# The S5 setup's and tables' transfers on GpSimd's queue instead of SyncE's

## The chip, the cores and the metric

The kernel runs on one core of a Trainium2 chip. A core has five engines that run side by side, each with its own in-order list of instructions: TensorE (PE in the profile; its weight loads are PEld), VectorE (DVE), ScalarE (ACT), GpSimd (POOL) and SyncE (SP). An engine that issues a DMA puts it into its own list; if that DMA has to wait for data or for a buffer, everything behind it in the list waits too. The metric is device microseconds for one execution, lower being better.

## The reference

One layer of a hybrid decoder over 2048 tokens of width 1024, in float32: an RMSNorm, one wide input projection, three branches and a gated merge.

```
h = rms_norm(x) * norm_w
ua, za, q, k, v, zb, xbc, dt, zc, g = split(h @ w_in)
ya = s5_mixer(ua, ...)                      # diagonal complex state space, 32 groups of 16 channels, 64 states
yb = dilated_window_attention(norm(q), norm(k), v)   # 3 pairs of (window, dilation)
yc = ssd(conv(xbc), dt, ...)                # chunked scan of Mamba-2
y  = sum(sigmoid(g_i) * (silu-gated y_i @ proj_i)) @ w_out + x
```

What the change touches belongs to `s5_mixer`. Its recurrence is linear, so that the response of a group to 8 steps of input can be tabulated from the parameters alone:

```
step = exp(log_step);  lam = exp((a_re + i a_im) * step)
bb = ((lam - 1) / a) * b
bu = einsum(bb, u);  h_t = lam * h_(t-1) + bu_t
y  = Re(c h) + d * u
```

Nothing in these tables depends on the tokens, only on `a`, `b`, `c`, `d` and `log_step`.

## The kernel before, in words

Every float32 matmul is done as three in the type fp32r: an operand is split into a high half (a cast on ACT, `wh_*`, `hT_hi`) and a low half (a subtraction on DVE, `wl_*`, `hT_lo`), and high × high, low × high and high × low are summed (L398 to L400 and L409 to L411). So PE needs four tensors made by ACT and DVE before it can go through a piece of the projection.

The 2048 tokens are handled in two halves of 1024. For each half the projections run over pieces of w_in's columns, and one matmul group is a unit. `main` (L1545 and on) hands side jobs to ranges of units: `s5_setup` to units 2 to 38, `s5_tables` to units 41 to 86, attention of the first half beside the tables, the first half's chunked scan (SSD) to units 89 to 135. PE's projection matmuls are the steady work that all side jobs hide behind.

The program's start is `a0` (L311): eight token tiles, each loaded as two DMAs (`load_x`, L280), squared on ACT (L289), its two sums added on DVE (L290), its inverse root taken on POOL (`rsqrt`, L248 and L249, tile `xs`), scaled on DVE (L297), transposed on PE (L301, `xT`), and split into `hT_hi` (ACT, L330) and `hT_lo` (DVE, L331). `consts` (L206 to L243) loads small constants, among them the convolution's weights `convw` (L241, L242, scaled on DVE in L243). `a0_early` does tiles 8 to 15 later, in the same way except that the result goes to DRAM (L343). The norms of the attention heads (`ss_q`, `ss_k`) use the same `rsqrt` on POOL, and their scaled results go out through L442.

`s5_setup` (L1066) loads the parameters (13 DMAs: four `s5ld`, one `s5prm`, four `s5b`, four `s5c`), computes powers and phases on DVE, and puts ten pieces into a DRAM table `tab_d` through the helper `put` (L1083), and `rho_d`. `s5_tables` (L1235) loads `s5dd` once and then goes through 16 blocks of two groups. A block loads its table rows (`s5t`, L1246), forms three complex products (`s5x`, `s5k`, `s5o`: two products each on POOL in L1261 and L1262, one sum on DVE in L1263), lets PE transpose `s5x` (`s5pp`, L1269) and multiply by `s5k` (`s5kp`, L1278), forms `s5w` (L1303 to L1305), and stores four results (`p_d`, `ks_d`, `o_d`, `wt_d`). The tile `s5t` has two buffers, so that a block's load can run one block ahead.

The order within each engine is not the order of the source text. The framework simulates the program on a timeline and writes each engine's list in the order in which that simulation issued the instructions; it also adds the waits. So a line that moves to another engine changes the order of all lists:

```
with tile.TileContext(nc, schedule_with_timeline_sim=True) as tc:
    Hybrid(tc, aps, out).build()
```

Completion of DMAs is signalled by eight semaphores for those that SP issues and another eight for those that POOL issues; a ninth transfer in flight waits for the first of its kind.

Of the kernel before, what the change touches and what calls it, by code (L numbers as in the profile page):

```python
# [21 lines left out]
P = 128  # L22
# [127 lines left out]
class Hybrid:  # L150
# [915 lines left out]
    def s5_setup(self):  # L1066


        nc, A = self.nc, self.A
        sm = Small(nc, self.jp, [P, 32])  # L1070
        prm = self.ct("s5prm", [P, 3, 32])
        ld = self.ct("s5ld", [32, 2, 2, 64])
        for i, w in enumerate(("s5_a_re", "s5_a_im")):
            for j in range(2):
                nc.sync.dma_start(ld[:, i, j, :], A[w][0])
        nc.sync.dma_start(prm[:, 2, :], A["s5_log_step"].partition_broadcast(P))
        pt = self.cps([P, 2, 32], "s5pt")
        for i in range(2):
            nc.tensor.transpose(pt[:, i, :], ld[:, i].rearrange("g j p -> g (j p)"), self.ident[:32, :32])
        nc.vector.tensor_copy(prm[:, 0:2, :], pt)  # L1080
        ar, ai = prm[:, 0, :], prm[:, 1, :]
        def put(off, wd, src):
            nc.sync.dma_start(self.tab_d[:, :, off * 2:(off + wd) * 2], src)  # L1083
        bb = [self.ct(f"s5b{i}", [P, 32, 16]) for i in range(2)]
        for i, (up, dn) in enumerate((("s5_b_re", "s5_b_im"), ("s5_b_im", "s5_b_re"))):
            nc.sync.dma_start(bb[i][0:64], A[up][0].rearrange("g p i -> p g i"))
            nc.sync.dma_start(bb[i][64:128], A[dn][0].rearrange("g p i -> p g i"))
        nc.vector.tensor_scalar(bb[1][0:64], bb[1][0:64], -1.0, None, op0=ALU.mult)
        yield
        step = sm.exp(prm[:, 2, :])  # L1090
# [2 lines left out]
        mag, cs, sn, fr, fi, ang, rho = (sv[:, i, :] for i in range(7))  # L1093
# [43 lines left out]
        mul(t, nr, ai)  # L1137
        sub(fi, fi, t)
        mul(fi, fi, den)
        nc.sync.dma_start(self.rho_d, rho)  # L1140
        w = self.ct("s5w", [P, 32, 18])
        nc.vector.tensor_copy(w[:, :, 0:9], lr)
        nc.vector.tensor_copy(w[:, :, 9:18], li)
        put(128, 18, w.rearrange("p (b g) k -> p b (g k)", b=16))
        w = self.ct("s5wr", [P, 32, 2, 8])
        for n in range(8):
            nc.vector.tensor_copy(w[:, :, 0, 7 - n], lr[:, :, n])
            nc.vector.tensor_copy(w[:, :, 1, 7 - n], li[:, :, n])
        put(146, 16, w.rearrange("p (b g) a n -> p b (g a n)", b=16))
        yield  # L1150

# [3 lines left out]
        for i in range(2):  # L1155
            o = self.ct(f"s5bb{i}", [P, 32, 16])
            t = self.ct(f"s5bt{i}", [P, 32, 16])
            mul(o, bb[i], b16(fr))
            mul(t, bb[1 - i], b16(fi))
            (sub if i else add)(o, o, t)  # L1160
            put(64 + 16 * i, 16, o.rearrange("p (b g) k -> p b (g k)", b=16))
        yield
        c = [self.ct(f"s5c{i}", [P, 4, 2, 64]) for i in range(2)]
        for i, w in enumerate(("s5_c_re", "s5_c_im")):
            src = A[w][0].rearrange("(b g) i p -> (g i) b p", g=8)
            nc.sync.dma_start(c[0][:, :, i, :], src)
            nc.sync.dma_start(c[1][:, :, 1 - i, :], src)
        nc.vector.tensor_scalar(c[0][:, :, 1, :], c[0][:, :, 1, :], -1.0, None, op0=ALU.mult)
        nc.vector.tensor_scalar(c[1], c[1], -1.0, None, op0=ALU.mult)
        for i in range(2):  # L1170
# [8 lines left out]
        for lev in range(2):  # L1179
# [5 lines left out]
            for k in range(7 if lev else 3):  # L1185
                if lev == 0 or k >= 3:
                    a, b = sm.t(), sm.t()
# [11 lines left out]
            n = 2  # L1199
            qr, qi = pr, pi  # L1200
            t = self.ct(f"s5pt{lev}", [P, 32, 16])
            while n < 16:
                a, b = sm.t(), sm.t()
# [31 lines left out]
    def s5_tables(self):  # L1235


        nc, A = self.nc, self.A
        v, gp = nc.vector, nc.gpsimd
        dd = self.tct("s5dd", [16, 32])  # L1240
        nc.sync.dma_start(dd, A["s5_d"][0].rearrange("(g i) -> i g", i=16))

        for b in range(16):
            gs = slice(b * 2, b * 2 + 2)
            w = self.tct(f"s5t{b}", [P, 2 * TABW], tag="s5tab", bufs=2)
            nc.sync.dma_start(w, self.tab_d[:, b, :])  # L1246

            def piece(off, wd=16):
                return w[:, off * 2:(off + wd) * 2].rearrange("p (g k) -> p g k", k=wd)
            pw, rev = piece(128, 18), piece(146)  # L1250
            b1, b2, d1, d2 = (piece(k) for k in (64, 80, 96, 112))

            def cplx(name, lr, li, x1, x2):

                o = self.tct(f"s5{name}{b}", [P, 2, 8, 16], tag="s5c", bufs=3)
                t = self.tct(f"s5{name}t{b}", [P, 2, 8, 16], tag="s5ct", bufs=2)

                def bc(k, x):
                    return (k.unsqueeze(3).to_broadcast([P, 2, 8, 16]),
                            x.unsqueeze(2).to_broadcast([P, 2, 8, 16]))  # L1260
                gp.tensor_mul(o, *bc(lr, x1))  # L1261
                gp.tensor_mul(t, *bc(li, x2))  # L1262
                v.tensor_add(o, o, t)  # L1263
                return o

            x1 = cplx("x", rev[:, :, 0:8], rev[:, :, 8:16], b1, b2)
            pp = self.cps([P, 2, P], f"s5pp{b}")
            for g in range(2):
                nc.tensor.transpose(pp[:, g, :], x1[:, g].rearrange("p n i -> p (n i)"), self.ident)  # L1269
            p1 = self.tct(f"s5p1{b}", [P, 2, P], tag="s5p1", bufs=1)  # L1270
            nc.scalar.copy(p1, pp)
            nc.sync.dma_start(self.p1_d[:, gs, :], p1)
            yield
            o0 = cplx("k", pw[:, :, 0:8], pw[:, :, 9:17], d1, d2)

            kp = self.cps([16, 2, P], f"s5kp{b}")
            for g in range(2):
                nc.tensor.matmul(kp[:, g, :], b1[:, g, :], o0[:, g].rearrange("p n i -> p (n i)"),  # L1278
                                 start=True, stop=True)
            ks = self.tct(f"s5ks{b}", [16, 2, 15, 16], tag="s5ks", bufs=1)  # L1280
            v.memset(ks[:, :, 0:7, :], 0.0)
            nc.scalar.copy(ks[:, :, 7:15, :].rearrange("p g n i -> p g (n i)"), kp)
            for g in range(2):
                v.scalar_tensor_tensor(ks[:, g, 7, :], self.ident[0:16, 0:16], dd[:, b * 2 + g:b * 2 + g + 1],
                                       ks[:, g, 7, :], op0=ALU.mult, op1=ALU.add)
            nc.sync.dma_start(self.ks_d[:, gs, :], ks.rearrange("p g n i -> p g (n i)"))
            yield
            o1 = cplx("o", pw[:, :, 1:9], pw[:, :, 10:18], d1, d2)
            nc.sync.dma_start(self.o1_d[:, gs, :], o1.rearrange("p g n i -> p g (n i)"))
            yield  # L1290
            wt = self.tct(f"s5w{b}", [P, 2, 2, 256], tag="s5w", bufs=1)
            tmp = self.tct(f"s5wt{b}", [P, 2, 256], tag="s5wt", bufs=1)

            def lo16(k):
                return piece(k).unsqueeze(2).to_broadcast([P, 2, 16, 16])

            def hi16(k):
                return piece(k).unsqueeze(3).to_broadcast([P, 2, 16, 16])

            def v16(a):  # L1300
                return a.rearrange("p g (a b) -> p g a b", b=16)
            for q, (x, y, f) in enumerate(((0, 16, v.tensor_sub), (16, 0, v.tensor_add))):
                gp.tensor_mul(v16(wt[:, :, q, :]), hi16(32), lo16(x))  # L1303
                gp.tensor_mul(v16(tmp), hi16(48), lo16(y))
                f(wt[:, :, q, :], wt[:, :, q, :], tmp)  # L1305
            nc.sync.dma_start(self.wt_d[:, gs], wt)
            yield

    def s5(self):
# [376 lines left out]
```

## Time and profile before

| what | value |
|---|---|
| median of 3 runs | 2508.95 us (2505.32 to 2513.44) |
| profiled execution | 2510.43 us |
| its span in the trace | 2508.4 us |
| mean granted clock of PE | 0.988 |
| DMA traffic | 457.65 MB in 449734 packets |
| DMAs of S5 setup and tables on SP's queue | 105 |

The profiled execution is one run; 2.0 us of its time lie around the span. The busy times of the engines count arithmetic only, so the time that an engine spends issuing a DMA is not in them. In the timeline a number in brackets at a row's end is the idle time of that engine just before the row, and the name behind it is what it waited for. "SPq" marks instructions of SP's list, DMA issues above all; the time in such a row is that of the issue, not of the transfer. "PEclk" is the share of PE's full clock that was granted in the stretch.

### The profile page before, as it was taken

The numbers are of one execution on the slowest core, as the hardware profiler recorded it, in microseconds if no ns is written. First come the engines' busy times: TensorE is split into PE (matmuls) and PEld (weight loads), VectorE is DVE, ScalarE is ACT, GpSimd is POOL, SyncE is SP. The second block draws the span as 40 slices with busy tenths as digits, with TensorE's granted clock in tenths as the row PEclk, the third lists the DMA queues.
The fourth block names the chain that finished last, engine by engine and source line by source line (L and its number), as shares of the span: only waits on it lengthen the run. The fifth ranks groups of instructions, "written<-read, shape, count | busy, mean of one in ns | idle before, by whom it ended". The sixth has DMA issues, their size and how long they took to land.

```text
span 2508.4 us, 40680 instructions
## 1 busy us (share of the span) xinstructions
PE 2426.4 (97%) x15072; PEld 2126.8 (85%) x15072; DVE 1436.5 (57%) x3104; ACT 836.6 (33%) x1780; POOL 722.8 (29%) x785
## 2 busy tenths in 40 slices
PE   8989999999999999999999999999999799999999
PEld 8989998788788888988999978878888578898888
DVE  6953467876767672577664566632334886552321
ACT  4223334543444343222243355542332312120100
POOL 2242233543344540245331000010110465422120
PEclk9999999999999999999999999999999899999999
DMA  7764543454544456466544567783343689898886
GB/s 165 111 166 139 163 124 128 139 168 131 155 140 123 125 170 195 113 183 169 156 154 140 166 204 211 239 269 106 114 130 108 209 281 314 292 304 292 297 285 221
DMA packets 449734, 457.65 MB, mean 182 GB/s; under 512 B 115585, under 2 KB 389505, under 8 KB 442369
## 3 DMA queue, kind: packets, MB, share of 16 engines
q1 hardware_dynamic: 449536, 455.06, 59.0%
q8 instruction: 119, 1.95, 0.3%
q14 instruction: 79, 0.64, 0.1%
HBM read 306.90 MB, written 148.06 MB: 181 GB/s over the span
## 4 chain that ended last, share of the span: by engine, by line
PE 68%; DMA 12%; DVE 10%; POOL 3%; SPq 3%; ACT 2%; issue 2%; ACTq 0%; DVEq 0%; POOLq 0%
PE fp L1500 3%; PE fp L1501 3%; PE fp L1502 3%; PE ps_g L410 3%; PE ps_g L409 3%; PE ps_g L411 3%; PE ao L874 2%; PE ps_uz L409 2%; PE ps_uz L411 2%; PE ps_uz L410 2%; PE op L1531 2%; PE op L1532 2%; PE op L1533 2%; PE psx_g L722 2%; PE psx_g L720 2%
## 5 line engine op out<-in xcount | busy, mean ns | idle before, releaser
L1013 POOL TENSOR_TENSOR sr<-tle,ahl 128x384 fp32r<-128x384 f32 x128 | 126.6, 1008 | 483.9 <-PE sd L1018 400.4
L1501 PE MATMUL fp<-fy_lo,fp 128*128 128x512 f32 x384 | 154.4, 402 | 6.5 <-DVE fy_lo L1473 6.5
L1500 PE MATMUL fp<-fy_hi,fp 128*128 128x512 f32 x384 | 156.7, 409 | 0.0
L409 PE MATMUL ps_g<-hT_hi,wh_g 128*128 128x512 f32 x384 | 155.4, 405 | 0.0
L410 PE MATMUL ps_g<-hT_lo,wh_g 128*128 128x512 f32 x384 | 154.3, 402 | 0.0
L411 PE MATMUL ps_g<-hT_hi,wl_g 128*128 128x512 f32 x384 | 154.1, 401 | 0.0
L1502 PE MATMUL fp<-fy_hi,fp 128*128 128x512 f32 x384 | 153.7, 400 | 0.0
L1531 PE MATMUL op<-fo,fm_hi 128*128 128x256 f32 x512 | 146.1, 286 | 4.7 <-DMA fo<-wo_d 4.7
L1505 POOL TENSOR_TENSOR fm<-fm,fg 128x512 f32<-128x512 f32 x64 | 86.7, 1355 | 218.1 <-DVE fg L1503 153.4
L1532 PE MATMUL op<-fo,fm_hi 128*128 128x256 f32 x512 | 144.8, 283 | 0.0
L1533 PE MATMUL op<-fo,fm_lo 128*128 128x256 f32 x512 | 144.5, 283 | 0.1
L409 PE MATMUL ps_xbc<-hT_hi,wh_xbc 128*128 128x512 f32 x320 | 130.0, 406 | 0.0
L411 PE MATMUL ps_xbc<-hT_hi,wl_xbc 128*128 128x512 f32 x320 | 128.9, 403 | 0.0
L410 PE MATMUL ps_xbc<-hT_lo,wh_xbc 128*128 128x512 f32 x320 | 127.9, 400 | 0.0
L853 ACT ACTIVATE sm<-sm,ml 128x256 f32<-128x256 f32 (+1 forms) x192 | 86.3, 451 | 119.9 <-DVE ml L851 113.5
L398 PE MATMUL ps_q<-wh_q,hT_hi 128*128 128x256 f32 x384 | 112.1, 293 | 7.5 <-ACT wh_q L385 7.4
L400 PE MATMUL ps_q<-wh_q,hT_lo 128*128 128x256 f32 x384 | 109.9, 287 | 3.9 <-DVE hT_lo L331 3.9
L399 PE MATMUL ps_v<-wl_v,hT_hi 128*128 128x256 f32 x384 | 108.5, 283 | 3.2 <-DVE wl_v L386 3.2
L399 PE MATMUL ps_q<-wl_q,hT_hi 128*128 128x256 f32 x384 | 110.0, 287 | 0.9 <-DVE wl_q L386 0.9
L398 PE MATMUL ps_v<-wh_v,hT_hi 128*128 128x256 f32 x384 | 109.6, 286 | 0.0
L398 PE MATMUL ps_k<-wh_k,hT_hi 128*128 128x256 f32 x384 | 108.7, 285 | 0.0
L399 PE MATMUL ps_k<-wl_k,hT_hi 128*128 128x256 f32 x384 | 108.2, 283 | 0.2 <-DVE wl_k L386 0.2
(477 smaller groups left out, 7579.5 us busy)
## 6 DMA issues: line engine op xcount, KB each, us to landing
fp<-pw_d SPq DMA_DIRECT2D x32, 1536.0 KB, 6.7
fo<-wo_d SPq DMA_DIRECT2D x16, 2048.0 KB, 9.0
fg<-g_d SPq DMA_DIRECT2D x96, 256.0 KB, 7.0
gr<-in_w_in_dram SPq DMA_DIRECT2D x48, 256.0 KB, 3.4
wr_g<-in_w_in_dram SPq DMA_DIRECT2D x12, 1024.0 KB, 5.4
g_d<-e_g SPq DMA_DIRECT2D x48, 256.0 KB, 2.4
wr_xbc<-in_w_in_dram SPq DMA_DIRECT2D x10, 1024.0 KB, 5.7
x<-in_x_dram SPq DMA_DIRECT2D x32, 256.0 KB, 3.7
```

Of the source, the lines that this page charges most:

```text
L398: nc.tensor.matmul(ps, hi[:, t], wh, start=kt == 0, stop=False)
L399: nc.tensor.matmul(ps, hi[:, t], wl, start=False, stop=False)
L409: nc.tensor.matmul(ps, wh, hi, start=kt == 0, stop=False)
L410: nc.tensor.matmul(ps, wh, lo, start=False, stop=False)
L411: nc.tensor.matmul(ps, wl, hi, start=False, stop=kt == KT - 1)
L1013: nc.gpsimd.tensor_mul(r, self.tle.unsqueeze(1).to_broadcast([P, 3, P]), ahl[:, i, h0:h0 + 3].unsqueeze(2).to_broadcast([P, 3, P]))
L1500: nc.tensor.matmul(ps, W[k][0], yh[k], start=k == k0, stop=False)
L1501: nc.tensor.matmul(ps, W[k][0], yl[k], start=False, stop=False)
L1502: nc.tensor.matmul(ps, W[k][1], yh[k], start=False, stop=k == k1 - 1)
L1531: nc.tensor.matmul(ps, mh[k][:, t], W[k][0], start=k == 0, stop=False)
L1532: nc.tensor.matmul(ps, mh[k][:, t], W[k][1], start=False, stop=False)
L1533: nc.tensor.matmul(ps, mlo[k][:, t], W[k][0], start=False, stop=k == 7)
```

## The change

Fourteen source lines name another engine for their DMA: eight in `s5_setup` (the parameter loads, `rho_d`, and `put`) and six in `s5_tables`. Written out over the loops these are 24 DMAs of the setup and 81 of the tables, 105 in all. No shape, no buffer and no arithmetic is changed.

```diff
         for i, w in enumerate(("s5_a_re", "s5_a_im")):
             for j in range(2):
-                nc.sync.dma_start(ld[:, i, j, :], A[w][0])
-        nc.sync.dma_start(prm[:, 2, :], A["s5_log_step"].partition_broadcast(P))
+                nc.gpsimd.dma_start(ld[:, i, j, :], A[w][0])
+        nc.gpsimd.dma_start(prm[:, 2, :], A["s5_log_step"].partition_broadcast(P))
...
         def put(off, wd, src):
-            nc.sync.dma_start(self.tab_d[:, :, off * 2:(off + wd) * 2], src)
+            nc.gpsimd.dma_start(self.tab_d[:, :, off * 2:(off + wd) * 2], src)
...
-            nc.sync.dma_start(bb[i][0:64], A[up][0].rearrange("g p i -> p g i"))
-            nc.sync.dma_start(bb[i][64:128], A[dn][0].rearrange("g p i -> p g i"))
+            nc.gpsimd.dma_start(bb[i][0:64], A[up][0].rearrange("g p i -> p g i"))
+            nc.gpsimd.dma_start(bb[i][64:128], A[dn][0].rearrange("g p i -> p g i"))
...
-        nc.sync.dma_start(self.rho_d, rho)
+        nc.gpsimd.dma_start(self.rho_d, rho)
...
-            nc.sync.dma_start(c[0][:, :, i, :], src)
-            nc.sync.dma_start(c[1][:, :, 1 - i, :], src)
+            nc.gpsimd.dma_start(c[0][:, :, i, :], src)
+            nc.gpsimd.dma_start(c[1][:, :, 1 - i, :], src)
...
-        nc.sync.dma_start(dd, A["s5_d"][0].rearrange("(g i) -> i g", i=16))
+        nc.gpsimd.dma_start(dd, A["s5_d"][0].rearrange("(g i) -> i g", i=16))
...
-            nc.sync.dma_start(w, self.tab_d[:, b, :])
+            nc.gpsimd.dma_start(w, self.tab_d[:, b, :])
...
-            nc.sync.dma_start(self.p1_d[:, gs, :], p1)
+            nc.gpsimd.dma_start(self.p1_d[:, gs, :], p1)
...
-            nc.sync.dma_start(self.ks_d[:, gs, :], ks.rearrange("p g n i -> p g (n i)"))
+            nc.gpsimd.dma_start(self.ks_d[:, gs, :], ks.rearrange("p g n i -> p g (n i)"))
...
-            nc.sync.dma_start(self.o1_d[:, gs, :], o1.rearrange("p g n i -> p g (n i)"))
+            nc.gpsimd.dma_start(self.o1_d[:, gs, :], o1.rearrange("p g n i -> p g (n i)"))
...
-            nc.sync.dma_start(self.wt_d[:, gs], wt)
+            nc.gpsimd.dma_start(self.wt_d[:, gs], wt)
```

What the new simulation made of it is seen in the engines' lists. The first place is the start of DVE's list, in `a0`. Before, the first scalings of `x` (tiles 0 and 1 in two halves each, `x_0` and `x_1`) come right behind the sums of squares:

```order
L216 CAST tgtr<-tgt 128x128
L290 TENSOR_TENSOR xs_173<-xs_173 128x1
L290 TENSOR_TENSOR xs_197<-xs_197 128x1
L297 SCALAR_TENSOR_TENSOR x_0_120<-x_0_120,xs_173,nwb 128x512
L297 SCALAR_TENSOR_TENSOR x_1_121<-x_1_121,xs_173,nwb 128x512
```

And now, the end of what stands ahead of the same scaling:

```order
L76 TENSOR_TENSOR sm_4_703<-sm_4_703,sm_3_700 128x32
L243 TENSOR_SCALAR convw<-convw 128x50
L77 TENSOR_TENSOR sm_4_703<-sm_4_703,sm_3_700 128x32
L78 TENSOR_TENSOR sm_4_703<-sm_4_703,sm_3_700 128x32
L79 TENSOR_SCALAR sm_4_703<-sm_4_703 128x32
L88 TENSOR_TENSOR sm_4_703<-sm_4_703,sm_7_722 128x32
L88 TENSOR_TENSOR sm_6_721<-sm_4_703,sm_8_727 128x32
L297 SCALAR_TENSOR_TENSOR x_0_120<-x_0_120,xs_173,nwb 128x512
```

The scaling of `x_0_120` went from the 12th place of the list to the 49th; the `sm` rows are the setup's exponential, which needs the `s5prm` load, and `convw` needs the last load of `consts`. On POOL the first rsqrt (`xs_173`) follows the constants' masks before, and now follows these rows:

```order
L1075 DMA s5ld<-in_s_a_im_dram 32x64 x2
L1076 DMA s5prm<-in_s_log_step_dram 128x32
L1086 DMA s5b_570<-in_s_b_re_dram 64x32x16
...
L1166 DMA s5c_1550<-in_s_c_im_dram 128x4x64
L1167 DMA s5c_1551<-in_s_c_im_dram 128x4x64
L518 MEMSET xb_cv_0_4950 128x3
L248 TENSOR_SCALAR xs_173<-xs_173 128x1
```

All thirteen parameter loads of S5 are ahead of it (the first two `s5ld` stand among the masks). The second place is the beginning of the tables, where token tile 9 (`x_0_2270`) is loaded on SP. Before:

```order
L442 DMA v_d_70<-e_v_0_1_2206 128x2x256
L1289 DMA o_d<-s5o_3825 128x256
L280 DMA x_0_2270<-in_x_dram 128x512
L280 DMA x_1_2271<-in_x_dram 128x512
```

And now on SP, with a store of normed keys (`e_k_1_1`) two places ahead of the load:

```order
L442 DMA k_d_67<-e_k_1_0_1990 128x2x256
L442 DMA v_d_70<-e_v_0_0_2154 128x2x256
L442 DMA k_d_67<-e_k_1_1_2049 128x2x256
L442 DMA v_d_70<-e_v_0_1_2206 128x2x256
L280 DMA x_0_2270<-in_x_dram 128x512
L280 DMA x_1_2271<-in_x_dram 128x512
```

The S5 store is gone from there. It stands on POOL now, ahead of the rsqrt of those keys (`ss_k_1_1`) and of that of tile 9 (`xs_2274`):

```order
L1289 DMA o_d<-s5o_3825 128x256
L1262 TENSOR_TENSOR s5kt_4014<-s5t_3918 128x256
L249 TENSOR_TENSOR ss_k_1_1_2051<-ss_k_1_1_2051,nhalf 128x8
L1306 DMA wt_d<-s5w_3909 128x1024
L1304 TENSOR_TENSOR s5wt_4248<-s5t_3918 128x512
L248 TENSOR_SCALAR xs_2274<-xs_2274 128x1
```

The third place is POOL's list in a block of the tables. Before, products follow products:

```order
L1261 TENSOR_TENSOR s5o_4453<-s5t_4256 128x256
L1262 TENSOR_TENSOR s5xt_4602<-s5t_4599 128x256
L1262 TENSOR_TENSOR s5kt_4696<-s5t_4599 128x256
L1303 TENSOR_TENSOR s5w_4802<-s5t_4599 128x2x256
L1304 TENSOR_TENSOR s5wt_4803<-s5t_4599 128x512
L1303 TENSOR_TENSOR s5w_4802<-s5t_4599 128x2x256
L1261 TENSOR_TENSOR s5x_4601<-s5t_4599 128x256
```

Now three DMAs stand between the same products:

```order
L1261 TENSOR_TENSOR s5o_4453<-s5t_4256 128x256
L1246 DMA s5t_4599<-tab_d 128x324
L1286 DMA ks_d<-s5ks_4021 16x480
L1289 DMA o_d<-s5o_4453 128x256
L1262 TENSOR_TENSOR s5xt_4602<-s5t_4599 128x256
L1262 TENSOR_TENSOR s5kt_4696<-s5t_4599 128x256
```

A block's load, its `ks_d` store and its `o_d` store moved in front of the next block's `s5xt`; `p_d` and `wt_d` stand further along, one each per block.

## Rows read from the trace of the kernel before

**Rows 1.** The page's first part: busy us, share of the span, instructions.

```profile
PE 2426.4 (97%) x15072; PEld 2126.8 (85%) x15072; DVE 1436.5 (57%) x3104; ACT 836.6 (33%) x1780; POOL 722.8 (29%) x785
```

**Rows 2.** Waits of PE, 0 to 330 us: waited for, total us, times, longest.

```profile
PE ps_q L398 <- ACT wh_q L385: 7.4, 2, 6.8
PE ps_q L400 <- DVE hT_lo L331: 3.9, 1, 3.9
```

**Rows 3.** Busy times by stretch: length, each engine's us (count), clock, DMA share, GB/s.

```profile
15.00:45.00 30.00, 25.51 (x198) 24.47 (x198) 22.41 (x51) 19.12 (x47) 9.53 (x16) 0.94 0.79 145
75.00:150.00 75.00, 71.60 (x601) 70.79 (x600) 64.01 (x306) 19.09 (x33) 19.97 (x18) 1.00 0.67 112
150.00:200.00 50.00, 42.75 (x340) 42.25 (x339) 23.06 (x59) 15.13 (x32) 23.39 (x30) 0.90 0.73 194
170.00:185.00 15.00, 7.75 (x41) 7.25 (x41) 8.05 (x11) 2.92 (x7) 10.06 (x13) 0.66 0.61 186
300.00:325.00 25.00, 21.56 (x175) 20.46 (x174) 21.51 (x64) 9.28 (x25) 9.44 (x12) 0.93 0.50 161
400.00:600.00 200.00, 198.16 (x1090) 159.47 (x1086) 141.53 (x296) 92.89 (x217) 92.71 (x114) 1.00 0.48 146
```

**Rows 4.** Timeline 0 to 36, by engine: start us, us, instruction, idle before it.

```profile
2.63 0.29 POOL L222 TENSOR_SCALAR_AFFINE_SELECT amask<-amask 128x128 f32<-128x128 f32 x1
...
10.08 2.74 DVE L297 SCALAR_TENSOR_TENSOR x<-x,xs,nwb 128x512 f32<-128x512 f32 x4 [1.05 <-POOL xs L249]
...
26.72 0.19 DVE L243 TENSOR_SCALAR convw<-convw 128x50 f32<-128x50 f32 x1 [3.90 <-DMA convw<-in_conv_b_dram]
...
15.93 0.28 PE L400 MATMUL ps_q<-wh_q,hT_lo 128*128 128x256 f32 x1
...
13.60 0.94 SPq L280 DMA_DIRECT2D x<-in_x_dram  x2
...
23.13 0.63 SPq L242 DMA_DIRECT2D convw<-in_conv_b_dram  x1
...
34.37 1.32 SPq L370 DMA_DIRECT2D wr_k<-in_w_in_dram  x1
```

**Rows 5.** DMA issues: operation, count, KB each, median us from issue to landing.

```profile
wr_k<-in_w_in_dram SPq DMA_DIRECT2D x6, 1024.0 KB, 6.5
...
o_d<-s5o SPq DMA_DIRECT2D x16, 128.0 KB, 2.3
...
tab_d<-s5bb SPq DMA_DIRECT2D x2, 256.0 KB, 11.4
...
s5b<-in_s_b_im_dram SPq DMA_DIRECT2D x2, 128.0 KB, 4.8
...
s5c<-in_s_c_im_dram SPq DMA_DIRECT2D x2, 128.0 KB, 6.8
```

**Rows 6.** Timeline 163 to 190, SP and ACT, where tile 9 is loaded.

```profile
171.97 0.32 SPq L1289 DMA_DIRECT2D o_d<-s5o  x1
172.34 0.92 SPq L280 DMA_DIRECT2D x<-in_x_dram  x2
...
176.20 0.60 ACT L289 ACTIVATE xj<-x 128x512 f32<-128x512 f32 x1 [11.03 <-DMA x<-in_x_dram]
```

**Rows 7.** Timeline of DVE and PE in two table blocks: sum s5x, then its transposes.

```profile
320.40 0.41 DVE L1263 TENSOR_TENSOR s5x<-s5x,s5xt 128x256 f32<-128x256 f32 x1
...
322.15 0.64 PE L1269 MATMUL s5pp<-ident,s5x 128*128 128x128 f32 x2
...
392.12 1.27 DVE L1263 TENSOR_TENSOR s5x<-s5x,s5xt 128x256 f32<-128x256 f32 x1 [1.10 <-POOL s5x L1261]
...
400.95 0.39 PE L1269 MATMUL s5pp<-ident,s5x 128*128 128x128 f32 x2
```

**Rows 8.** Timeline of DVE, 380 to 402: one sum of 128x512, twice.

```profile
389.48 1.53 DVE L1305 TENSOR_TENSOR s5w<-s5w,s5wt 128x512 f32<-128x512 f32 x1 [0.72 <-POOL s5wt L1304]
...
395.00 0.68 DVE L1305 TENSOR_TENSOR s5w<-s5w,s5wt 128x512 f32<-128x512 f32 x1
```

## The prediction, made before the changed kernel was run

> **What bounds the kernel now.** I read the page's busy times first: TensorE (PE) is busy 97% of the span and every other engine under 60% [rows 1]. So the time changes only where PE sits idle or runs at a reduced clock, and the question is which of those places the moved transfers touch. PE's waits before 330 us, the stretch in which S5 setup and tables run, name the worst two: weights that ACT casts late, and a low half hT_lo that DVE makes late [rows 2]. The busy times by stretch size them [rows 3]. I charge a stretch its idle time plus (1 − granted clock) × busy time:
> - 15 to 45: 4.5 idle + 0.06 × 25.5 = 1.5, so 6.0;
> - 75 to 150: 3.4 idle at full clock;
> - 150 to 200: 7.25 idle + 0.10 × 42.75 = 4.3, so 11.5, of which 170 to 185 alone has 7.25 + 0.34 × 7.75 = 9.9;
> - 300 to 325: 3.4 + 1.5 = 4.9;
> - 400 to 600, eight table blocks: 1.8 in 200, so there PE hardly waits.
>
> The timeline of several engines shows the causes. At the start the first scaling of x runs at 10.08 and PE has its first full set of inputs at 15.93; the later hole ends when DVE, which stood at convw's scaling for 3.9 us until the conv_b load landed, gets on [rows 4]. At 172 the S5 store o_d, which waited on SP for DVE's sum, has the next x loads behind it; ACT sits 11 us until they land [rows 6].
>
> **The change part by part.** 105 DMAs leave SP for POOL, 24 of setup and 81 of tables (1 + 5 × 16). No arithmetic changes, but all engines get a new order, and that order is where I find the cost.
>
> *Start: +12.* Thirteen S5 loads now stand on POOL ahead of the first rsqrt. On DVE, 37 more instructions stand ahead of the first x scaling, among them convw's. So the first scaling now waits for the conv_b load. SP reaches that load without two pairs of x loads (the pair shown takes 0.94, so about 1.9): 23.13 − 1.9 = 21.2. From issue to DVE took 26.72 − 23.13 = 3.6, so convw comes at 24.8, and behind five small DVE operations x at about 25.8, 15.7 later than now [rows 4]. The first hT_lo further waits for the low half of wr_k, loaded behind conv_b: 21.2 + 0.63 + 6.5 landing [rows 4, 5] = 28.3, then two casts of ACT, two subtractions of DVE and hT_lo itself, some 4 us: PE is fed at about 32.5 instead of 15.93, +16.5. The hole of 6.0 between 15 and 45 is the same wait for convw and is not paid twice: −6. A PE that has been idle comes back at a lower clock (2.6 lost in 170 to 185 [rows 3]): +2. Sum +12.
>
> This holds while POOL is through its thirteen DMAs before 24.3, the scaling less 1.5 for the rsqrt. It is free at 2.9 [rows 4], so they may take 21.4 in all, 1.65 each. No row has a DMA on POOL. From below: SP's issue of conv_b, 0.63 [rows 4], gives 8 us. From above, if POOL were held until the data land: 4 × 4.8 + 4 × 6.8 for the B and C matrices, 5 × 2.3 for the small ones [rows 5], 58 us. I take 1.6, about the geometric middle of 0.63 and the 4.5 mean of the upper end, as issuing is nearer in kind to the 0.63; that is just hidden. Ends: +8, if the convw wait is shorter on the emptier queue, and +48 (58 of DMAs end at 61, the scaling comes at 62 instead of 25.8).
>
> *Stretch 75 to 330: −8.* Its losses are 3.4 + 11.5 + 4.9 = 19.8. With S5's stores off SP, the x loads of tile 9 no longer stand behind o_d, which frees most of the 9.9. But the new order puts that tile's rsqrt on POOL behind the same o_d store and a wt_d store, and the x loads on SP behind a k_d store whose rsqrt is also behind o_d. So a part comes back on POOL. I take 8 of the 19.8. Ends: −20 and +5 (two stores at their landing of 2.3 [rows 5] ahead of the rsqrt, nothing freed). The Trainium skill (DMA: Bandwidth & Descriptors, "Issuing engines are not separate DMA queues") says that issuing from several engines saves only the sequencer's time to initiate, usually small beside the transfer; by it this term would be 0 and the sum 2526. The row speaks against it: what held SP was o_d's wait for DVE, not its issue of 0.32 [rows 6].
>
> *Tables: +4.* In each block three DMAs (s5t, ks_d, o_d) now stand between two of POOL's products, ahead of s5x. Their price lengthens POOL's chain to PE's transposes s5pp. At 1 us each (between 0.32 for SP's o_d [rows 6] and its landing of 2.3 [rows 5]; half-way, as these are small) it is +3 per block. The slack from the end of the s5x sum to s5pp is 400.95 − 393.39 = 7.6 in one block and 322.15 − 320.81 = 1.3 in the tightest I saw [rows 7]. Two or three tight blocks of 16 lose 1.7 each: +4. Ends: 0, and +22 (2.3 each, four tight blocks at 6.9 − 1.3).
>
> *Puts, rho_d, s5dd: 0.* The ten puts meet a POOL that is busy 20 us of 75 and 23 of 50 [rows 3]; its idle time covers them at 1 to 2 us each. If they held it for their landing, 11.4 [rows 5], ten would take 114 and the cover is gone (rival B). The end of the tables and all behind 620 us: 0, as only the order is shuffled there.
>
> Sum: 12 − 8 + 4 = +8 on the profiled execution's 2510.4, **2518 us**. That execution lies 1.5 above the median of 2508.95, within the runs' spread of 8.
>
> **The rivals.**
> - **B, POOL's price is large.** A DMA on POOL costs well over 1.65 us. For: nothing in the trace shows POOL issuing one, and the B and tab_d transfers are cut into the smallest pieces, landing in 4.8 and 11.4 against o_d's 2.3 [rows 5]. Against: SP issues within 0.32 to 1.32 [rows 4, 6]. At 40 us for the thirteen loads x comes at 44.5: +19 over my start; tables +13 instead of +4: 2518 + 28 = 2546. At the upper ends 2580.
> - **C, faster.** SP's relief is whole (−20), POOL's stores cost the tables nothing, the start is at its +8: 2498. It decides at tile 9: if ACT's 11 us [rows 6] vanish and no wait on POOL's rsqrt takes their place. Against it: the rsqrt's new place.
> - **D, a draw.** Start +12, relief −15, tables +2: −1, so 2509. For it: PE's losses in 75 to 330 are of the size of the start's loss.
> - **E, DVE and POOL in each other's way.** The same DVE sum of 128x512 takes 0.68 alone and 1.53 when POOL's product runs beside it [rows 8], 0.85 more. If each of 105 DMAs on POOL met DVE so, 105 × 0.85 = 89 us; a quarter of it on PE, mostly in the tables, gives +22 over my sum: 2540. The Trainium skill (SBUF — State Buffer, "SBUF: two separate sides", the "DVE blocks DMA" trap) says that a DMA issued from GpSimd has its descriptors written by GpSimd, which is locked out while DVE runs a two-port operation. The rows show the mutual slowing of arithmetic; none shows a DMA on POOL.
> - If POOL's DMAs went through the same queue at SP's price, the change would do less than it says; the start's +12 stays, since it comes from DVE's order. That is inside A and D.
>
> **How the numbers follow.** My forecast A 0.42, B 0.20, C 0.13, D 0.18, E 0.07. A measurement of this kernel can tell about 0.3%, 7.5 us, from no change: 2501.4 to 2516.5 is "same". A lies above that edge by 2 us only, so a third of it, 0.13, counts as same. Faster: C, 0.13. Same: D 0.18 + 0.13 of A = 0.31. Slower: 0.29 of A + B + E = 0.56. The range runs from 2500, leaving out half of C (0.07), to 2556, leaving out the dearer half of B (0.10). Cases of both signs are in it; A's own range is 2510 to 2530.
>
> **What would show it.** The start: first x scaling near 26, behind convw, and PE's first low-half product near 32; if the scaling waits for POOL's rsqrt instead, B holds. POOL's DMA rows: near or under 1.65 us each at the start, near 1 in the tables. Stretch 150 to 200: idle and clock loss near 4 instead of 11.5; a wait of ACT for x or of DVE for the rsqrt in its place speaks against C. Tables: PE waits for s5x only in single blocks. A second queue on the page would show that POOL's DMAs go another way. The prediction is wrong if the first x scaling comes before convw, if POOL's DMAs take several us each, or if PE's losses from 75 to 330 stay or grow.

## The result and the profile after

| | before | changed |
|---|---|---|
| median | 2507.31 us (4 runs) | 2529.03 us (4 runs, 2520.91 to 2530.80) |
| ratio | | 1.0080, 95% interval 1.0066 to 1.0093 |
| profiled execution's span | 2508.4 us | 2527.2 us |

The change is slower by 0.8%, some 20 us: inside the range, on the side that was forecast, and 11 us above the 2518. On the chip that ran most of the experiments it was 1.0086 (1.0070 to 1.0102). One execution of a later kernel (B loads in pieces), 2955.72 us, is in the slow state and is left out of that kernel's ratio.

The changed kernel's page, its first and third part (busy times; queue, packets, MB, share of the DMA engines): PE does the same work in a longer span, POOL has 105 instructions more, and there is a second kind of queue, which the kernel before did not have.

```profile
PE 2427.6 (96%) x15072; PEld 2126.4 (84%) x15072; DVE 1448.0 (57%) x3104; ACT 836.5 (33%) x1780; POOL 788.1 (31%) x890
...
q1 hardware_dynamic: 407792, 435.55, 55.0%
q0 software_dynamic: 6544, 19.51, 2.9%
```

The changed kernel's busy times in the stretches of [rows 3]:

```profile
15.00:45.00 30.00, 8.56 (x41) 7.75 (x42) 17.56 (x58) 9.89 (x24) 2.07 (x5) 0.56 0.74 161
75.00:150.00 75.00, 75.00 (x638) 75.00 (x637) 68.39 (x323) 21.22 (x36) 33.44 (x29) 1.00 0.61 127
150.00:200.00 50.00, 47.47 (x387) 46.82 (x386) 26.12 (x60) 15.34 (x30) 29.31 (x37) 0.97 0.58 176
170.00:185.00 15.00, 14.93 (x122) 14.69 (x121) 8.79 (x12) 4.63 (x11) 14.12 (x17) 0.96 0.69 239
300.00:325.00 25.00, 25.00 (x216) 24.07 (x215) 17.18 (x55) 9.38 (x26) 12.94 (x19) 1.00 0.56 175
400.00:600.00 200.00, 198.90 (x1106) 159.27 (x1105) 146.06 (x300) 92.93 (x219) 112.66 (x156) 1.00 0.45 141
```

From 15 to 45 us PE now works 8.6 of 30 us. From 150 to 200 it idles 2.5 us and loses 0.03 × 47.5 = 1.4 to the clock, 4 instead of 11.5; 300 to 325 is full, with the loss moved behind it. The tables are as busy as before.

The changed kernel's timeline at the start (start, us, instruction), of POOL, ACT, SP, DVE and PE:

```profile
2.30 1.25 POOL L1075 DMA_DIRECT2D s5ld<-in_s_a_re_dram  x2
...
5.61 1.14 POOL L1086 DMA_DIRECT2D s5b<-in_s_b_re_dram  x1
...
12.54 0.76 POOL L1167 DMA_DIRECT2D s5c<-in_s_c_im_dram  x1
...
14.04 1.10 POOL L249 TENSOR_TENSOR xs<-xs,nhalf 128x1 f32<-128x1 f32 x2
...
21.62 2.18 ACT L385 CAST wh_q<-wr_q 128x512 fp32r<-128x512 f32 x4 [12.43 <-DMA wr_q<-in_w_in_dram]
...
11.70 2.59 SPq L227 DMA_DIRECT2D qkw<-in_k_norm_w_dram  x1
21.61 0.47 SPq L227 DMA_DIRECT2D qkw<-in_q_norm_w_dram  x1
...
29.26 0.68 SPq L242 DMA_DIRECT2D convw<-in_conv_b_dram  x1
...
32.57 0.19 DVE L243 TENSOR_SCALAR convw<-convw 128x50 f32<-128x50 f32 x1 [3.04 <-DMA convw<-in_conv_b_dram]
...
33.66 2.74 DVE L297 SCALAR_TENSOR_TENSOR x<-x,xs,nwb 128x512 f32<-128x512 f32 x4
...
41.73 0.56 PE L400 MATMUL ps_q<-wh_q,hT_lo 128*128 128x256 f32 x1
```

POOL is through its thirteen DMAs at 13.3 and has two rsqrts at 15.1: it holds nobody up. But wr_q, which ACT casts, lands at 21.6, and SP issues nothing from 14.3 to 21.6, with eight transfers in flight. So conv_b goes out at 29.26 (forecast 21.2), and x is scaled at 33.66, behind convw as forecast, 7.9 later than forecast. PE's first low-half product comes at 41.73 (forecast 32.5).

The DMA issues of the first 36 us say why (KB each, us to landing), first of the kernel before:

```profile
wr_q<-in_w_in_dram SPq DMA_DIRECT2D x1, 1024.0 KB, 9.1
```

and of the changed kernel:

```profile
wr_q<-in_w_in_dram SPq DMA_DIRECT2D x1, 1024.0 KB, 17.8
...
s5b<-in_s_b_re_dram POOLq DMA_DIRECT2D x2, 128.0 KB, 9.1
...
s5c<-in_s_c_re_dram POOLq DMA_DIRECT2D x2, 128.0 KB, 9.3
```

wr_q was issued at 3.8 in both. The S5 loads, which stood behind conv_b before, now run beside wr_q, and all get in each other's way: between 10 and 15 us the kernel before moved 364 GB/s, the changed one 153, with the DMA engines busy throughout (share 1.00 and 1.13; the kernel before is the first row):

```profile
10.00:15.00 5.00, 3.50 (x17) 3.27 (x17) 4.67 (x8) 2.43 (x5) 0.00 (x0) 0.66 1.00 364
10.00:15.00 5.00, 0.00 (x0) 0.00 (x0) 0.00 (x0) 0.00 (x0) 4.45 (x9) 0.59 1.13 153
```

**How far PE is behind.** To see where time is lost I took, from two traces, the start of the same matmul (same tiles, same place in their count) and its difference, and the median of these over a stretch. The base is a second profile of the kernel before ("before again", an execution of 2501.64 us). Positive is later, in us; each row is one profiled execution against that one. That of only tables on POOL was the slowest of its twelve executions (2514.79, median 2509.98).

| kernel | 60 to 80 | 250 to 300 | 650 to 700 | 1800 to 1900 | from 2400 |
|---|---|---|---|---|---|
| before, first profile | −0.8 | 5.0 | 5.3 | 9.1 | 8.7 |
| change, first profile | 18.5 | 15.2 | 18.9 | 19.8 | 27.2 |
| change, again | 19.4 | 15.3 | 18.6 | 19.9 | 24.6 |
| only the 13 loads on POOL | 16.3 | 19.2 | 20.6 | 22.4 | 27.2 |
| all but the loads on POOL | −0.8 | −2.2 | 0.4 | −0.1 | 10.0 |
| only tables on POOL | −0.8 | −0.2 | 3.0 | 4.4 | 11.7 |
| tables but p_d on POOL | −0.6 | −2.8 | 2.6 | 2.0 | −2.3 |
| only p_d on POOL | −1.3 | −0.6 | 0.8 | −0.2 | 2.9 |
| only puts on POOL | −2.4 | −0.4 | −0.2 | 5.9 | 3.0 |

So the change loses 18.5 at the start, gains 3.3 by 250, loses 3.7 in the tables, 0.9 up to 1900 and 7.4 in the last 500 us. The row of the first profile shows how far one execution of the same kernel can be off: 5.8 us by 250, in the stretch of tile 9 and ahead of it, and 4 between 1000 and 1700. "Only puts" jumps by 6 near 1200, where nothing was edited.

### The profile page after: what moved, and what is told of

It reads as the page before. It is cut to its first block, busy times and chain, and to the rows that moved or that the text cites. A ratio compares the mean times of both kernels' runs of the same rounds, so it can differ in the third digit from the quotient of the medians.

```text
span 2527.2 us, 40664 instructions
## 1 busy us (share of the span) xinstructions
PE 2427.6 (96%) x15072; PEld 2126.4 (84%) x15072; DVE 1448.0 (57%) x3104; ACT 836.5 (33%) x1780; POOL 788.1 (31%) x890
## 4 chain that ended last, share of the span: by engine, by line
PE 72%; DMA 11%; DVE 8%; SPq 3%; issue 2%; POOL 2%; ACT 2%; DVEq 0%; ACTq 0%; POOLq 0%
PE ps_g L410 3%; PE ps_g L409 3%; PE ps_g L411 3%; PE fp L1500 3%; PE fp L1501 2%; PE fp L1502 2%; PE ao L874 2%; PE ps_xbc L409 2%; PE ps_xbc L411 2%; PE ps_xbc L410 2%; PE op L1533 2%; PE op L1531 2%; PE op L1532 2%; PE psx_g L722 2%; PE psx_g L720 2%
## 5 line engine op out<-in xcount | busy, mean ns | idle before, releaser
L1500 PE MATMUL fp<-fy_hi,fp 128*128 128x512 f32 x384 | 157.5, 411 | 5.7 <-DVE fg L1503 4.0
L1531 PE MATMUL op<-fo,fm_hi 128*128 128x256 f32 x512 | 145.5, 285 | 1.7 <-DMA fo<-wo_d 1.7
L527 DVE SCALAR_TENSOR_TENSOR ac_cv<-xb_cv,convw,ac_cv 128x512 f32<-128x512 f32 x120 | 99.3, 829 | 25.3 <-ACT ac_cv L525 24.5
L400 PE MATMUL ps_v<-wh_v,hT_lo 128*128 128x256 f32 x384 | 109.3, 285 | 0.0
```

The costliest lines, as they stand in the source:

```text
L400: nc.tensor.matmul(ps, lo[:, t], wh, start=False, stop=kt == KT - 1)
L1500: nc.tensor.matmul(ps, W[k][0], yh[k], start=k == k0, stop=False)
L1531: nc.tensor.matmul(ps, mh[k][:, t], W[k][0], start=k == 0, stop=False)
```

## The experiments

Theory 1, made from this: early S5 transfers clog the DMA engines and delay wr_q and all that SP issues behind it; the move of stores off SP gains a little; what the tables cost is small. Rival, theory 2: each DMA costs POOL time that PE then waits for. The ratios below come from two chips, each against the kernel before on the same chip: the tables, p_d alone and before again ran on one (median before 2503.9), all others on the other (2501.4 and 2503.2).

**The loads back on SP, and the loads alone.**

```diff
 # the change, but with the thirteen loads of s5_setup as before
-            nc.gpsimd.dma_start(bb[i][0:64], A[up][0].rearrange("g p i -> p g i"))
+            nc.sync.dma_start(bb[i][0:64], A[up][0].rearrange("g p i -> p g i"))
```

> The thirteen parameter loads are issued by SP again; puts, rho_d and all table transfers stay on POOL. Theory 1 (the loss is the start's: the early loads share the DMA engines with wr_q, and x stands behind convw on DVE): wr_q lands near 13 us, first x scaling near 10, PE's progress at 100 us as before (within 2 us), the 10 us gained between 150 and 200 kept, tables +1 to +4: 2500 to 2506, faster than before or level. Theory 2 (each DMA on POOL costs POOL time that PE waits for, also in the tables): the 92 DMAs left on POOL cost most of the loss, 2515 or more.

> Only the thirteen parameter loads go to POOL; puts and tables stay on SP. Theory 1: the start's loss whole, PE 19 us behind at 60 to 150 us, the stall near tile 9 as in before, so 2524 to 2532. Theory 2: a start like before's within 5 us, since thirteen issues took POOL only 10.5 us, and no table loss: 2506 to 2512.

Measured: with the loads back 1.0033 (1.0019 to 1.0046), first x scaling at 9.80, wr_q landing 9.0 after its issue; the loads alone 1.0126 (1.0106 to 1.0146), x at 33.03, wr_q in 17.7. The thirteen loads make nearly the whole loss of the start (16.3 of 18.5 to 19.4), as theory 1 has it. But it had the first of the two level or faster, and it was 8 us slower: the table shows it level up to 1900 and 10 behind at the end. That part was unexplained, and neither theory had it. The loads alone also did not keep the stall near tile 9 as expected: PE's wait for wh_q there is gone, and one of 6.8 for wl_v stands ahead of it. And they cost more than the whole change (1.0126 against 1.0086), so the other 92 DMAs give something back beside them.

**The loads on POOL, but late.** A tiny POOL copy from convw into each target tile holds the loads until convw is there.

```diff
+        cp(ld[:, :, 0, 0], cw[0:32, 0, 0:2])
+        cp(prm[:, 2, 0:1], cw[:, 0, 0:1])
...
+            cp(bb[i][:, 0, 0:1], cw[:, 0, 0:1])
...
+            cp(c[i][:, 0, :, 0], cw[:, 0, 0:2])
```

> As the change, but six tiny POOL copies from convw into the loads' target tiles make the thirteen loads wait until convw is there, near 25 us, still on POOL. Theory 1: wr_q lands near 13, x is scaled near 10, PE's progress at 100 us within 3 us of before, the tile 9 gain kept: 2499 to 2508. Theory 2: thirteen DMAs of 0.6 to 1.1 us on POOL stand ahead of the rsqrts of the later tiles and of the first head norms: PE 8 to 12 us behind at 100 us, 2512 or more.

Measured: 1.0040 (1.0023 to 1.0056). wr_q landed in 8.9 and x was scaled at 9.74, as theory 1 had it, but PE was 6.7 us behind at 60 to 80, near theory 2. This kernel's timeline of POOL, and of DVE behind it:

```profile
32.48 0.57 POOL L248 TENSOR_SCALAR xs<-xs 128x1 f32<-128x1 f32 x1
33.11 1.15 POOL L1092 DMA_DIRECT2D s5b<-in_s_b_re_dram  x1
...
39.75 0.77 POOL L1175 DMA_DIRECT2D s5c<-in_s_c_im_dram  x1
40.51 0.65 POOL L249 TENSOR_TENSOR xs<-xs,nhalf 128x1 f32<-128x1 f32 x1
...
43.55 0.29 DVE L1176 TENSOR_SCALAR s5c<-s5c 128x256 f32<-128x256 f32 x1 [1.33 <-DMA s5c<-in_s_c_im_dram]
43.76 2.74 DVE L297 SCALAR_TENSOR_TENSOR x<-x,xs,nwb 128x512 f32<-128x512 f32 x4
```

Eight DMAs, 7.4 us, stand between the two halves of one rsqrt, which theory 2 would have as the cause. But the second of the two rsqrts that the scaling needs is done at 42.7, and DVE comes to the scaling at 43.76, behind the setup's exponential and a row that waited 1.33 for an s5c load. So late loads on POOL do cost time at the start, by POOL's list and by DVE's place behind what they load; how much each of the two costs is not shown.

**More transfers in the kernel before, in small pieces or in runs.** The kernel before loads the B matrices a second time on POOL, at the start, into tiles that nothing reads; a second version reads the same bytes in runs of 2 KB per partition.

```diff
+            xb = self.ct(f"xb{i}", [P, 32, 16])
+            nc.gpsimd.dma_start(xb[0:64], A[up][0].rearrange("g p i -> p g i"))
+            nc.gpsimd.dma_start(xb[64:128], A[dn][0].rearrange("g p i -> p g i"))
 # second version
+            nc.gpsimd.dma_start(xb[0:64], A[up][0].rearrange("g (a p) i -> (g a) p i", a=2))
```

> The kernel before, with four more loads on POOL at the start: the S5 B matrices a second time, into tiles that nothing reads. x stays ahead of convw on DVE. Theory 1 (transfers on the DMA engines delay wr_q): wr_q lands 3 to 6 us later than 13, PE's first products later by as much, start lag +3 to +8, 2510 to 2516. If DVE's order alone made the loss and the transfers did not matter: wr_q at 13, lag under 3 (POOL's four issues of 1.1 us end before 8 us), within 3 us of before.

> As the kernel before with the four additional B loads on POOL, but each partition reads one run of 2 KB instead of 32 pieces of 64 bytes; the bytes are the same, the tiles are again read by nothing. If the small pieces hold the DMA engines: wr_q within 2 us of its 9 us landing, start lag under 3 us, within 4 us of before. If any early load on POOL does it, whatever its pieces: wr_q near 16.5 us, lag near 8, 10 to 15 slower, as with the pieces.

Measured: in pieces 1.0080 (1.0053 to 1.0108), in runs 1.0019 (1.0010 to 1.0029); PE at 60 to 80 is 8.4 and 1.9 behind. DMA of the first 36 us, in pieces:

```profile
q0 software_dynamic: 192, 0.52, 10.0%
...
wr_q<-in_w_in_dram SPq DMA_DIRECT2D x1, 1024.0 KB, 16.5
xb<-in_s_b_re_dram POOLq DMA_DIRECT2D x2, 128.0 KB, 10.3
```

and in runs:

```profile
q0 software_dynamic: 192, 0.52, 5.5%
...
wr_q<-in_w_in_dram SPq DMA_DIRECT2D x1, 1024.0 KB, 11.1
xb<-in_s_b_re_dram POOLq DMA_DIRECT2D x2, 128.0 KB, 7.0
```

The same 192 packets and 0.52 MB hold the DMA engines nearly twice as long, and wr_q lands 5.4 us later. This kernel has x ahead of convw on DVE, so the order cannot be the cause. It is the small pieces, and half of the change's B and C loads is enough for 8 us at the start. Not only wr_q is late with the pieces (by 7.4, where 3 to 6 were expected): the first x scaling comes at 15.87, after DVE waited 4.24 for nwb, another load of SP. With the pieces the kernel is 20 us slower, over the 2510 to 2516 of theory 1; its profiled execution, the fastest, is 6.2 behind at 1800 to 1900 and 13.3 at the end, the rest of which the last group of experiments takes up. The 1.0019 in runs is 5 us, a little over what was expected.

**The place behind convw.** The halving of the convolution weights is left out, with the order otherwise as in the change.

```diff
-        nc.vector.tensor_scalar(self.convw, self.convw, 0.5, None, op0=ALU.mult)
```

> The change without DVE's halving of the convolution weights (left out, so the convolution uses doubled weights); all else has the change's order, so the first x scaling no longer stands behind the conv_b load. If the delayed transfers make the start's loss: x scaling at 30 to 31 instead of 33.7 (it still stands behind wl_q and the setup's exponential), wr_k lands as before, start lag 15 to 19 us: 0 to 4 faster than the change. If the place behind convw makes it, as the prediction had it: x scaling near 15 to 18, lag under 8, 10 or more faster than the change.

> The change itself, on the chip of these runs. Every theory: start lag 18 to 19 us, 19 to 21 at 1900 us, and by the sum of the parts measured alone (loads 20, last stretch 4 to 10) 22 to 30 us slower than before.

Measured: 1.0095 (1.0075 to 1.0114) and, for the change, 1.0086 (1.0070 to 1.0102). Without the halving x is scaled here:

```profile
30.33 2.74 DVE L297 SCALAR_TENSOR_TENSOR x<-x,xs,nwb 128x512 f32<-128x512 f32 x4
```

3.3 earlier, and PE is 18.1 behind instead of 19.4. The place behind convw was the last link, not the cause: ahead of the scaling also stand the low half of wr_q and the setup's exponential, hardly earlier, and the first hT_lo then waits behind the low half of wr_k (36.57, in the change 37.12), whose load SP issues late. The change's 21 us are a little under the 22 to 30 expected.

**Tables, with and without the shuffled end.** With all 92 DMAs other than the loads on POOL time was lost at the end of the program, where nothing was edited. PE's rows in the traces show that most edits also shuffle its order from the 12,188th of 15,072 rows on (2004 us, in the last 500). The tables without p_d and the puts alone do not.

```diff
 # s5dd, s5t, ks_d, o_d and wt_d on POOL; in the other version p_d, too
-            nc.sync.dma_start(w, self.tab_d[:, b, :])
+            nc.gpsimd.dma_start(w, self.tab_d[:, b, :])
```

> The kernel before, unchanged, for a profile on the chip of these runs. Every theory: a time within the runs of before. Where its profile differs from the first one in the last 500 us, the difference there is the run's and not an edit's; where it agrees to 2 us, the last stretch of an edit can be compared with it.

> Table transfers on POOL except the 16 p_d stores: 65 DMAs; the setup's 24 and p_d stay on SP. In this build the order on PE is that of before from the 5000th instruction on. Theory A (the change's loss is the start's loads plus a shuffled order in the last 500 us, while the move of the table stores gains 7 to 10 us near tile 9): 2 to 9 us faster than before. Theory B (DMAs on POOL cost the tables time, 1 us each on its chain): 5 to 10 us slower than before.

> All 81 table transfers on POOL, the setup on SP. Beside the kernel with p_d on SP it differs by 16 stores, and by the order of the last 500 us, which is shuffled here. Theory A: 7 us ahead of before at 1900 us, as the other, and 8 to 15 lost behind it: 3 to 8 us slower than before. Theory B: like the other kernel with 16 more DMAs on POOL, within 3 us of it.

> Only the 16 p_d stores go to POOL; everything else stays on SP. The order of the last 500 us is shuffled as in the kernel with all tables on POOL; in the tables only few places differ. Theory A: no difference above 3 us up to 1900 us, then 8 to 15 lost in the last 500: 6 to 15 us slower than before, though 16 small stores cannot cost that. Theory B: 16 stores of 0.8 us that nothing waits for: within 3 us of before.

> Only the ten tab_d puts and rho_d go to POOL. The order on PE is that of before from the 1300th instruction on. The prediction's term was 0: POOL's idle time covers them. Within 3 us of before, also if they land late; if they held POOL for their landing of 6 to 11 us each, PE would be 5 us or more behind between 60 and 150 us.

Measured: before again 2501.64; tables without p_d 1.0001 (0.9987 to 1.0015); all tables 1.0017 (1.0007 to 1.0028); p_d alone 1.0017 (1.0004 to 1.0031); puts alone 0.9999 (0.9988 to 1.0010). The tables without p_d were expected 2 to 9 faster and are level, so the gain near tile 9 is smaller than in the first profiles: 2.2 in the table. Nor is the version with all tables 7 us ahead at 1900; its profile is 4.4 behind. The last stretch, from the first matmul fp of L1500 to the last op of L1531 (PE rows by tile: ns least, median, longest; us of the first and last start), in the kernel before, again:

```profile
L1531 PE MATMUL op<-fo,fm_hi x512: 274/283/576, 2079.3 to 2495.4; 128*128 128x256 f32 x171
```

```profile
L1500 PE MATMUL fp<-fy_hi,fp x384: 391/397/922, 1969.2 to 2449.2; 128*128 128x512 f32 x192
```

with all tables on POOL:

```profile
L1531 PE MATMUL op<-fo,fm_hi x512: 274/283/415, 2082.7 to 2507.1; 128*128 128x256 f32 x171
```

```profile
L1500 PE MATMUL fp<-fy_hi,fp x384: 392/397/1202, 1973.7 to 2460.8; 128*128 128x512 f32 x192
```

That is 526.2 and 533.4 us. In the same way, in the old order: the first profile of before 525.7, tables without p_d 521.7, puts alone 523.2. Two shuffled orders come back in kernels that have little else in common. The change (533.4, again 530.8), the loads alone (530.9) and the change without halving (532.4) have one; the change without its loads (536.3), all tables, p_d alone (529.0) and the B loads in pieces (533.2) have the other. In all of these PE waits in that stretch for fm_lo, a low half that DVE makes, 4.3 to 5.7 us, which is 0.2 or absent in the old order; here that of p_d alone (waited for, us, times, longest):

```profile
PE op L1533 <- DVE fm_lo L1513: 5.6, 1, 5.6
```

So these two orders cost 8 us on average (532.4 against 524.2), and the times agree: all tables is 6.6 us slower by its medians (2509.98 and 2503.35) than the version that leaves p_d on SP, and p_d alone, 16 stores that nothing waits for, is 0.17% slower, less than expected. The moved p_d stores are not the cause, as the loads alone and the B loads in pieces leave them on SP and take 530.9 and 533.2. Not every shuffle costs time: the held loads and the B loads in runs have orders of their own and take 524.4 and 526.9. Why fm_lo comes later in the two orders is not shown.

No version beat the kernel before. The tables without p_d come nearest, and are level.

## Why the prediction was right, and where it was off

The sum stood on the first profile of before. Against that one the table's five steps are +19.3, −9.1, +3.4, −2.9 and +7.8, where the forecast had +12, −8, +4, 0 and 0: the gap is made by the start and the end, less what the steps between give back. The figures below are against the second profile where nothing else is said.

- **Start, +12; measured 18.5.** The side was right and the chain too: x behind convw on DVE. The step that failed is "SP reaches that load without two pairs of x loads: 21.2". SP reached it at 29.26, as wr_q took 17.8 us to land and SP stood. I priced POOL's *issuing* of the thirteen DMAs and never what their *transfers* do to the others once they come 21 to 26 us earlier. With 29.26 in place of 21.2 the sum gives 12 + 8 = 20. And without convw's place the start is only 1.3 better, so my cause was one of several links.
- **POOL's price, 1.6 taken.** Too high: 0.50 to 1.14 at the start, so POOL was free at 13.3, far ahead of my limit of 24.3. With the loads held, POOL stood in front for 7.4 us, but DVE's wait for s5c ended later.
- **75 to 330, −8.** Measured −3.3 against the second profile of before and −9.1 against the one that I used (stretch 150 to 200 from 11.5 to 4). ACT's wait for x is gone, and one of 10.7 for wr_q stands in its place. Part of the 19.8 was one execution's: the second profile has no hole in 75 to 150, where I had 3.4, and 6.0 idle + 0.07 × 44.0 = 9.1 in 150 to 200 instead of 11.5. And my reason, S5's stores off SP, does not carry the term. Where the stores move and the loads stay on SP the same step is −1.4 (loads back), −2.2 (tables without p_d) and +0.6 (all tables), and ACT still waits for x there (10.9 to 15.4 us from 140 to 200, before again 21.7). Why the early loads and the moved stores together gain more is not shown.
- **Tables, +4.** Measured 3.7, and that is luck. No row of PE waits for s5x in the changed kernel's tables; the longest wait that grew is one for DVE's e_uz, from 2.3 to 3.8. The loss does come with the table DMAs (2.6 to 5.4 in the table's kernels that move 65 or 81 of them, 0.2 to 1.4 in the others), by a way that is not shown. The price of a DMA was 1 in my sum, and it is 0.58, with which three would pass the tightest slack of 1.3 by 0.4 and two or three blocks would lose about 1. First PE's wait for e_uz from 280 to 660 us in before again, then its three longest waits there in the changed kernel, then the DMAs on POOL:

```profile
PE ps_uz L409 <- DVE e_uz L486: 2.3, 1, 2.3
```

```profile
PE ps_uz L409 <- DVE e_uz L486: 3.8, 1, 3.8
PE ap L862 <- ACT sm L853: 3.1, 2, 2.6
PE ps_zc L399 <- DVE wl_zc L386: 1.6, 1, 1.6
```

```profile
L1246 POOL DMA_DIRECT2D s5t<-tab_d x16: 543/584/636, 158.0 to 602.0; - x16
```

```profile
L1289 POOL DMA_DIRECT2D o_d<-s5o x16: 542/587/630, 174.5 to 620.2; - x16
```

- **Puts, 0.** Right: alone they are level, though in the change each takes POOL 1.14 to 1.27 us and 7 to 10 to land.
- **All behind 620 us, 0.** Wrong by 5 to 8 us: "only the order is shuffled there" was the reason given, and both orders that the change and its parts got cost time.
- **Rivals.** B's condition (over 1.65 us per DMA) did not come about; that the start lost more than my sum did, for another reason. C fell at the start, D at its sum. E: POOL's table DMAs took 0.51 to 0.64 (s5dd once, 0.71) with DVE busy 73% of 400 to 600, so no row shows a DMA on POOL held up by DVE there. The Trainium skill (DMA: Bandwidth & Descriptors, "Issuing engines are not separate DMA queues") says that DMAs from any issuing engine run on the same 16 DMA engines and interleave there. The runs agree: the tables' o_d lands in 2.7 us from POOL and 2.3 from SP, and at the start the loads on POOL's queue delayed wr_q on SP's. What the new issuer changed at the start was the place in time: the loads came earlier, and that made 16 to 19 us.

## What to carry to other kernels

A transfer that moves to an idle queue also moves in time: ask not only what its issue costs, but which transfer on the critical path it will now share the DMA engines with, and how small its pieces are. Where a scheduler orders the program, compare the lists of the untouched stretches too: a reordered end can cost a quarter or more of what the edit does (here 5 to 8 of 20 us). And take a stall's size from more than one execution before it becomes a term.

## What the runs showed that I had not expected

Four loads of 128 KB in pieces of 64 bytes, issued by POOL, lengthened another queue's 1 MB load from 9.1 to 16.5 us; in runs of 2 KB, to 11.1. Two orders of PE's list, found in three and in four kernels with different edits, cost some 8 us in a stretch that no edit touched. The issue on POOL itself also depends on the pieces: 1.08 to 1.29 us each for the first, 0.52 to 0.75 for the second.
